# A hybrid GLA and RWKV-7 layer on one core: two small products in fp32 with four column groups, and a new set of precedences

## The chip, the cores and the metric

The kernel runs on one core of a Trainium2 chip. The metric is device time in microseconds (us) of one execution; less is better. The engines carry the profile's names: PE (TensorE: PE the matmuls, PEld the weight loads), DVE (VectorE), ACT (ScalarE), POOL (GpSimd) and SP (SyncE, which only issues DMAs here). SBUF is the on-chip memory of 128 partitions; PSUM holds matmul results, in eight banks of 128 partitions by 512 fp32 numbers.

A *product* below is one matmul instruction: a stationary block of up to 128x128 is loaded, and up to 512 moving columns stream past it. *f32r* is the kernel's fast reading of fp32 numbers, which keeps fewer bits. Where full precision is wanted, the kernel splits a number into a high part and a rest (hi + lo), both f32r, and adds up the products of the parts. An unsplit *fp32* product appears in the trace as two matmul records.

## What is computed

One layer over a prompt of 1024 tokens and eight sample tokens (one new token each for eight sequences), 1024 features. The part of the reference that the change touches:

```python
p = jnp.einsum('btd,dn->btn', x, w_in)
p_gla, p_rwkv, p_gate = _split(p, (GLA_COLS, RWKV_COLS, GATE_COLS))
q, k, v, g_a, a_lr = _split(p_gla, GLA_SPLITS)            # a_lr: 16 columns
log_a = jax.nn.log_sigmoid((jnp.einsum('btr,rk->btk', a_lr, gla_alpha_w2) + gla_alpha_b)
                           .astype(jnp.float32)) / GLA_TAU
...
m = (jax.nn.sigmoid(gate_a) * jnp.einsum('btc,cd->btd', o_gla, w_up_gla)
     + jax.nn.sigmoid(gate_b) * jnp.einsum('btc,cd->btd', o_rwkv, w_up_rwkv))
out = jnp.einsum('btd,de->bte', m, w_out)
y_out = _layernorm(DEEPNORM_ALPHA * x + out, ln_g, ln_b, LN_EPS)
```

`a_lr` is the low-rank factor of GLA's decay: 16 columns of `w_in` applied to x. `out` is the last product, over all prompt and sample tokens. Everything else (the chunked GLA, the RWKV-7 recurrence, gates, norms, states) is there too, and the change leaves it as it is.

## The kernel before

The tokens go through in two passes (`PASS`): pass 0 has 512 prompt tokens and the eight sample tokens, in tiles of 256 and 264 columns; pass 1 has the other 512 in one tile. x lies transposed, as eight blocks (k = 0 to 7) of 128 features by the pass's tokens, each split into `xh` and `xl`. A projection block is 128 output columns: for each tile, 8 blocks k times three f32r products (hi·xh, hi·xl, lo·xh), summed in one PSUM bank. Its weights come through `wraw`, are split by ACT (hi) and DVE or POOL (lo) into `wpart`, and in pass 0 are also written to DRAM, from where pass 1 reads them split.

Behind the projections run the heads and pairs: four GLA heads and eight RWKV pairs in each pass, with many small fp32 matmuls, then two up-projections, a merge and the product with `w_out`. PSUM's banks are named `proj` (2), `big` (5) and `pch` (1). SBUF scratch is mostly the 40 buffers called `row`.

The program is written by a scheduler of its own, `Order`. Each piece of work is a generator (a stream) that yields instructions; `run` keeps an estimated time for each engine and takes the instruction whose estimated start, less a precedence for its kind (`PRIO`, and for PE `FOR_PE`, with the weights `STAND`, `SCARCE`, `PER_ROW`, `URGENT`), is the earliest. `AGE`, `BIAS` and `ASIDE` are further weights in that choice, and `price` gives each instruction an estimated cost. What comes out is one fixed order of instructions for each engine; on the chip the engines wait for each other by semaphores. All instructions are issued by one helper, so most rows of the profile bear the line L227; the tiles' names tell them apart.

Two parts matter here:

- `low_rank` makes `a_lr`. Its weight `wa` (1024x16) is loaded into a `row`, zeroes are written over the final tile, and DVE makes the two parts: of each 128x16 block the stationary has 66 columns, of which 0 to 15 are the high part and 32 to 47 the rest. Each tile takes 16 products, 8 blocks times xh and xl, of 66 columns; ACT or DVE copies rows 0 to 15 of the bank, DVE adds rows 32 to 47, and the sum is split again into `alr` for the heads. It starts when all eight blocks of x are split.
- `out_sample` multiplies the sample rows with `w_out`. ACT gathers xh and xl of the last columns into a 96-column stationary block for each k, and 2 x 16 products of 512 columns run against the two parts of `w_out` (`self.wo`), which `load_out` has split for the prompt's rows. `out_part` adds two strips of the bank, rows 32 to 63 and 64 to 95, to the residual and does the layer norm. In `out` it stands behind the first of four row groups of pass 0; a row group (128 tokens) is 48 products of 512 columns.

A raw block of x is freed as soon as both its parts are made (`low` in `load_x`).

Of the kernel before, what the change touches and what calls it, by code (L numbers as in the profile page):

```python
# [66 lines left out]
RANKW, RANKM = 48, 66  # L67
# [10 lines left out]
AGE = 1.045  # L78
# [3 lines left out]
BIAS = 0.193  # L82
ASIDE = 8.388

PRIO = {"evacuate": 0.39, "pair": 0.3, "turn": 0.5, "chain": 0.42, "norm": 0.1, "x": 0.61, "lora": 0.42, "rank":
        1.25, "head": 0.27, "gate": -0.38, "w": 0.3, "out": 0.04, "state": -0.13, "block": -0.38}
FOR_PE = {"pair": 1.0, "turn": 1.84, "chain": 0.8, "norm": 0.39, "lora": 0.29, "rank": 1.85, "head": 0.89, "gate":
        1.0, "state": 2.11, "out": 0.05}
STAND, SCARCE, PER_ROW = 0.034, 0.249, 0.148

URGENT = 1.707
# [61 lines left out]
def price(eng, name, out, args, ins):  # L153
# [3 lines left out]
    if eng == "P":  # L157
        m = args[0].free_size()
        rows, cols = tiles(name, args)
        if name == "transpose":  # L160
            return 0.1095
        if args[0].dtype == F32R:
            return max(m / 1200, 0.0045 + n / 2256) if rows == cols == P else (m + n) / 1200
        if rows == cols == P:
            return 2 * max(m, n) / 1200 + 0.009
        return 0.1365 if cols == P else (0.0625 if cols == 64 else 0.142 if n > P else 0.088) if rows == P else 0.0625 if rows == cols == 64 else 0.5
# [264 lines left out]
class Kern(Order):  # L431
# [71 lines left out]
    def setup(self):  # L503
# [51 lines left out]
        self.wa = cp.tile([P, NK * RANKW + RANKM - RANKW], F32R, name="wa")  # L555
# [31 lines left out]
    def load_constants(self):  # L587
        a, V, E = self.a, self.V, self.E
        row, wa = yield from self.rows(2)
        wa = wa[:, :NK * 16]  # L590
        yield from self.load("pv", self.S.dma_start(self.pv, a["pv"]))
        yield from self.load("wa", self.S.dma_start(wa, a["wa"]))
# [5 lines left out]
        yield V.tensor_copy(self.wa, row[:, :NK * RANKW + RANKM - RANKW])  # L598
        hi, lo = (self.wa[:, :NK * RANKW].rearrange("p (k c) -> p k c", c=RANKW)[:, :, o:o + 16] for o in (0, 32))
        wa3 = wa.rearrange("p (k c) -> p k c", c=16)  # L600
        yield V.tensor_copy(hi, wa3)
        yield V.tensor_sub(lo, wa3, hi.bitcast(F32))
        self.free(wa)
        self.has.add("wa")
# [21 lines left out]
    def load_x(self, src, i, wait=None, low_rank=False):  # L626
# [5 lines left out]
        self.xq.append(xs)  # L632
        if low_rank:
            self.spawn(self.low_rank(self.ctx[i], xs), "rank")
# [8 lines left out]
        def low():  # L643
            for k in range(NK):
                yield lambda: len(his) > k
                lo = yield from self.get(f"xl{k}")
                yield self.E.tensor_sub(lo[:, :n], raws[k], his[k].bitcast(F32))
                self.free(raws[k])
                xs.append((his[k], lo[:, :n]))
        self.spawn(high(), "x")  # L650
# [149 lines left out]
    def low_rank(self, c, xs):  # L800

        yield lambda: len(xs) == NK and "wa" in self.has
        x_ = yield from self.row(c.n)
        for t0, n in c.tiles:
            q = yield from self.bank("big", [P, n])
            for k in range(NK):
                for v in range(2):
                    yield self.P.matmul(q[:RANKM], self.wa[:, RANKW * k:RANKW * k + RANKM], xs[k][v][:, t0:t0 + n],
                                        start=(k == v == 0), stop=(k == NK - 1 and v == 1))
            x = x_[0:16, t0:t0 + n]  # L810
            yield self.C.copy(x, q[0:16])
            yield self.V.tensor_add(x, x, q[32:48])
# [769 lines left out]
    def load_out(self):  # L1582
# [9 lines left out]
        for k in range(NK):  # L1592
# [21 lines left out]
            self.wo.append([[y.bitcast(F32R) for y in x] for x in parts])  # L1614

    def out(self, c, xs):


        rows = [(n * P, c.i * HT + n * P) for n in range(HT // P)]
        for t0, x0 in rows:  # L1620
            if t0 == P and c.ns:
                yield from self.out_sample(xs)
            fin = t0 == rows[-1][0]
            z, st, done = yield from self.residual(x0, P)
# [26 lines left out]
    def out_sample(self, xs):  # L1651

        W, M = 32, 96
        z, st, done = yield from self.residual(T - W, W)
        xs_ = yield from self.rows(2, NK // 2 * M)
        x3 = [x.bitcast(F32R).rearrange("p (k m) -> p k m", m=M) for x in xs_]
        for k in range(NK):
            yield lambda: len(xs) > k
            y = x3[k // 4][:, k % 4]
            yield self.C.copy(y[:, 0:64], xs[k][0][:, HT + NS - 64:])  # L1660
            yield self.C.copy(y[:, 64:M], xs[k][1][:, HT + NS - W:])
        for j in range(2):
            ps = yield from self.get_of("proj", "big")
            for k in range(NK):
# [4 lines left out]
            if j:  # L1669
                self.free(*xs_)  # L1670
            self.spawn(self.out_part(j, 2, z, j, slice(0, 512), [ps[32:64], ps[64:96]], st, TP, [ps], done), "evacuate")
# [108 lines left out]
    def run_all(self):  # L1780
# [5 lines left out]
        self.plan, self.xq, self.ws, self.wo, self.gts, self.l2s = [], [], [], [], [], []  # L1786
# [71 lines left out]
```

## Time and profile before

| | |
|---|---|
| median of 3 runs | 1460.86 us (1459.19 to 1461.2) |
| span of the profiled execution | 1457.3 us |
| total of the profiled execution | not listed; the median less the span is 3.6 us |
| DMA | 319.14 MB, mean 219 GB/s |
| DVE's costliest group | 191.1 us, 369 adds and products of rows |
| ACT's table loads | 54 in 69.3 us |

The profile gives for each engine the share of the span in which it is busy, and the span in 40 slices with the share in tenths. For a group or a piece of the timeline a row has the start in us and the duration, the engine, the source line, what is written and read (`big<-xh,wa` is a matmul into a `big` bank from `xh` and `wa`), the stationary's size (128*66), the moving operand's size, and the number of merged instructions (x2). In brackets stands how long the engine sat idle before it and what ended that. Matmuls are pipelined: a record's duration reaches into the next one's, so the cost of a stream of matmuls is read from start to start. A row of the windows view has the stretch, its length, then each engine's busy time with its count, the granted PE clock, DMA's share and GB/s.

### The profile page before, as it was taken

How to read it: one execution, taken by the hardware profiler on the slowest of the kernel's cores; microseconds unless marked ns; L12 is line 12 of the kernel's file. 1: busy time of each engine (PE TensorE's matmuls, PEld its weight loads, DVE VectorE, ACT ScalarE, POOL GpSimd, SP SyncE). 2: the span in 40 equal slices, each digit the busy share in tenths (PEclk: the TensorE clock that was granted, in tenths of full speed). 3: DMA queues.
4: the chain of work that ended last, by engine and by line, in shares of the span. 5: the costliest groups of instructions: out<-in, count | busy, mean ns of one | idle time of the engine just before them, and what ended most of it. 6: DMA issues, size and time to landing. Idle time of an engine off the chain costs nothing.

```text
span 1457.3 us, 30477 instructions
## 1 busy us (share of the span) xinstructions
PE 1443.5 (99%) x10768; PEld 1280.5 (88%) x10768; DVE 1058.8 (73%) x2208; ACT 828.9 (57%) x2114; POOL 362.6 (25%) x1111
## 2 busy tenths in 40 slices
PE   9999999999999999999999999999999999999997
PEld 8999999999999998878888888888788898898786
DVE  6687487958895889577747895787669856665665
ACT  5656667766776677455555565464557646643210
POOL 1060506050604160406051405411332330000000
PEclk9999999999999999999999999999999999999999
DMA  8786887678767885675466455746575768798432
GB/s 308 262 289 201 287 275 269 202 245 297 253 209 241 277 307 191 190 210 186 137 205 208 152 173 175 229 138 207 185 230 156 226 206 249 250 311 287 135 119 84
DMA packets 211315, 319.14 MB, mean 219 GB/s; under 512 B 91699, under 2 KB 107196, under 8 KB 211164
## 3 DMA queue, kind: packets, MB, share of 16 engines
q1 hardware_dynamic: 211164, 317.20, 67.6%
q8 instruction: 86, 1.41, 0.4%
q14 instruction: 65, 0.53, 0.1%
HBM read 197.45 MB, written 118.61 MB: 217 GB/s over the span
## 4 chain that ended last, share of the span: by engine, by line
PE 92%; DVE 3%; DMA 3%; ACT 1%; issue 1%; SPq 1%; DVEq 0%; ACTq 0%
PE proj L227 59%; PE big L227 27%; PE pch L227 6%; DVE row L227 1%; SPq L227 1%; DVE xl L227 0%; DMA wraw<-w_in 0%; DMA wide<-LD 0%; DVE wpart L227 0%; DMA row<-xT 0%; DMA wraw<-w_up_gla 0%; DMA row<-o_gla 0%; DMA wide<-Sp 0%; DVE XT L227 0%; DMA w<-wpart 0%
## 5 line engine op out<-in xcount | busy, mean ns | idle before, releaser
L227 PE MATMUL proj<-xh,wpart 128*128 128x264 f32 (+2 forms) x3696 | 901.3, 328 | 0.0
L227 PEld LDWEIGHTS proj<-xh,wpart 128*128 128x128 f32 x3696 | 614.2, 188 | 49.0 <-issue 6.5
L227 PE MATMUL proj<-xl,wpart 128*128 128x264 f32 (+2 forms) x1848 | 603.8, 327 | 0.0
L227 PEld LDWEIGHTS proj<-xl,wpart 128*128 128x128 f32 x1848 | 348.1, 188 | 23.6 <-issue 1.4
L227 POOL TENSOR_TENSOR Xt<-X,wide 128x60 f32<-128x60 f32 (+24 forms) x496 | 170.9, 344 | 676.5 <-DMA wide<-LD 281.4
L227 DVE TENSOR_TENSOR row<-row 128x256 f32<-128x256 f32 (+10 forms) x369 | 191.1, 530 | 14.6 <-ACT row L227 8.0
L227 DVE TENSOR_TENSOR wpart<-wraw,wpart 128x512 fp32r<-128x512 f32 x210 | 146.1, 698 | 74.4 <-ACT wpart L227 71.2
L227 ACT CAST wpart<-wraw 128x512 fp32r<-128x512 f32 x210 | 130.0, 621 | 100.1 <-PE proj L227 57.6
L227 POOL TENSOR_TENSOR X<-X,Xt 128x60 f32<-128x60 f32 (+24 forms) x496 | 170.3, 343 | 38.7
L227 ACT ACTIVATE row<-row 128x520 f32<-128x520 f32 (+4 forms) x229 | 137.7, 612 | 13.3 <-DMA row<-sg 5.6
L227 PE MATMUL big<-xh,wpart 128*128 128x256 f32 (+2 forms) x576 | 133.0, 320 | 0.2 <-DVE wpart L227 0.2
L227 PEld LDWEIGHTS big<-xh,wpart 128*128 128x128 f32 x576 | 95.3, 188 | 7.4 <-DVE wpart L227 0.4
L227 DVE TENSOR_TENSOR wide<-pch,gg 64x65 f32<-64x65 f32 x224 | 49.8, 222 | 65.1 <-PE pch L227 62.9
L227 ACT COPY row<-big 128x128 f32<-128x128 f32 (+6 forms) x152 | 49.7, 356 | 81.1 <-PE big L227 77.0
L227 PE MATMUL big<-xl,wpart 128*128 128x256 f32 (+2 forms) x288 | 92.2, 320 | 0.8 <-DVE xl L227 0.8
L227 DVE SCALAR_TENSOR_TENSOR row<-proj,pv,row 128x255 f32<-128x255 f32 (+1 forms) x95 | 54.6, 575 | 48.2 <-ACT tail L227 36.4
L227 ACT COPY rh<-pch 128x130 f32<-128x130 f32 x121 | 32.5, 268 | 98.8 <-PE pch L227 98.0
L227 ACT COPY wide<-pch 64x65 f32<-64x65 f32 x241 | 50.1, 208 | 50.4 <-PE pch L227 47.4
L227 ACT ACTIVATE row<-proj,omu 128x256 f32<-128x256 f32 (+1 forms) x95 | 52.2, 549 | 33.5 <-PE proj L227 32.5
L409 ACT ACT_TABLE_LOAD x54 | 69.3, 1283 | 0.9
L227 PE MATMUL big<-row 128*64 128x64 f32 (+4 forms) x648 | 65.0, 272 | 0.2 <-DVE gg L227 0.2
L227 PEld LDWEIGHTS big<-xl,wpart 128*128 128x128 f32 x288 | 54.2, 188 | 5.3 <-DVE xl L227 1.8
(234 smaller groups left out, 2069.6 us busy)
## 6 DMA issues: line engine op xcount, KB each, us to landing
w<-wpart SPq DMA_DIRECT2D x146, 512.0 KB, 4.3
wpart<-w SPq DMA_DIRECT2D x146, 512.0 KB, 3.8
wraw<-w_in SPq DMA_DIRECT2D x146, 256.0 KB, 4.2
wide<-LD SPq DMA_DIRECT2D x64, 128.0 KB, 3.8
wraw<-w_up_gla SPq DMA_DIRECT2D x32, 256.0 KB, 3.7
wraw<-w_up_rwkv SPq DMA_DIRECT2D x32, 256.0 KB, 3.7
sg<-row SPq DMA_DIRECT2D x16, 260.0 KB, 3.2
row<-sg SPq DMA_DIRECT2D x16, 260.0 KB, 4.3
```

Of the source, the lines that this page charges most:

```text
L227: ways.append((eng, lambda call=call: call(out, *args, **kw), price(eng, name, out, args, ins)))
L409: self.nc.scalar.preload_act_table_set(self.table)
```

## The change

Four things change.

`low_rank` works on unsplit fp32: `wa` is loaded straight into its tile, with 16 columns a block, and the moving operand is the raw block of x. Block k goes to column group k mod 4, that is to rows 0, 32, 64 or 96 of the bank, so four products stand in four groups of 32 columns of the array, and a second four adds to them. The four strips are then summed, by one copy and three adds. Pass 0 issues both tiles in one piece, once all eight raw blocks are there, into two `proj` banks; pass 1 issues two pieces of four blocks, into a `big` bank that it takes at its start. A raw block of x is freed only when low rank has used it.

```diff
-        self.wa = cp.tile([P, NK * RANKW + RANKM - RANKW], F32R, name="wa")
+        self.wa = cp.tile([P, NK * RANK], F32, name="wa")
...
-        yield V.tensor_copy(self.wa, row[:, :NK * RANKW + RANKM - RANKW])
...
-        yield V.tensor_copy(hi, wa3)
-        yield V.tensor_sub(lo, wa3, hi.bitcast(F32))
...
-    def low_rank(self, c, xs):
-
-        yield lambda: len(xs) == NK and "wa" in self.has
+    def low_rank(self, c, raws, ranked):
+
         x_ = yield from self.row(c.n)
-        for t0, n in c.tiles:
-            q = yield from self.bank("big", [P, n])
-            for k in range(NK):
-                for v in range(2):
-                    yield self.P.matmul(q[:RANKM], self.wa[:, RANKW * k:RANKW * k + RANKM], xs[k][v][:, t0:t0 + n],
-                                        start=(k == v == 0), stop=(k == NK - 1 and v == 1))
-            x = x_[0:16, t0:t0 + n]
-            yield self.C.copy(x, q[0:16])
-            yield self.V.tensor_add(x, x, q[32:48])
+        step = NK if c.i == 0 else 4
+        qs = []
+        for _, n in c.tiles:
+            qs.append((yield from self.bank("big" if c.i else "proj", [P, n])))
+        for k0 in range(0, NK, step):
+            yield lambda: len(raws) >= k0 + step and "wa" in self.has
+            yield together([self.P.matmul(q[g:g + RANK], self.wa[:, RANK * k:RANK * k + RANK], raws[k][:, t0:t0 + n],
+                                          start=(k < 4), stop=(k >= NK - 4), skip_group_check=True)
+                            for q, (t0, n) in zip(qs, c.tiles) for k in range(k0, k0 + step) for g in [k % 4 * 32]])
+            ranked[k0:k0 + step] = [True] * step
+        for q, (t0, n) in zip(qs, c.tiles):
+            x = x_[0:RANK, t0:t0 + n]
+            yield self.C.copy(x, q[0:RANK])
+            for g in range(32, P, 32):
+                yield self.V.tensor_add(x, x, q[g:g + RANK])
             self.free(q)
```

The sample rows do the same: `sample_rows` adds xh and xl of 32 columns back to fp32, the eight blocks are stationary in four groups, and `w_out` is loaded a second time, raw, in two halves of eight `row` buffers (`self.wr`). The sample rows now stand behind two row groups of pass 0 in place of one.

```diff
+        for j in range(2):
+            raws = yield from self.rows(NK, 512)
+            for k in range(NK):
+                yield self.S.dma_start(raws[k], self.a["w_out"][k * P:(k + 1) * P, 512 * j:512 * j + 512])
+            self.wr.append(raws)
...
-            if t0 == P and c.ns:
-                yield from self.out_sample(xs)
...
+            if t0 == 2 * P and c.ns:
+                yield from self.out_sample(ys)
...
-            for k in range(NK):
-                yield lambda: len(self.wo) > k
-                for v in range(2):
-                    yield self.P.matmul(ps[:M], x3[k // 4][:, k % 4], self.wo[k][v][j], start=(k == v == 0),
-                                        stop=(k == NK - 1 and v == 1))
...
+            qs = [ps[g:g + W] for g in range(0, P, W)]
+            yield together([self.P.matmul(qs[k % 4], ys[1][:, k], raws[k], start=(k < 4), stop=(k >= 4), skip_group_check=True)
+                            for k in range(NK)])
```

`price` gets a cost for the new form, and the precedences and weights get new values, two of them here:

```diff
-AGE = 1.045
+AGE = 1.137
...
-URGENT = 1.707
+URGENT = 1.514
```

So the order of all engines is laid out anew, and it differs at nearly every place behind the first 50 rows of PE. The following rows are of PE, at the three places of low rank and the sample rows (a row: line, operation, written and read tiles, size of the result; the number in `xh_239` counts tiles).

PE at the start, before the change: the first two projection blocks go through x block by block, and low rank's 66-column products stand behind eight of the twelve products of block 4 (six are left out here).

```order
L227 MATMUL big<-xh_237,wpart 128x264
L227 MATMUL big<-xh_252,wpart 128x256
L227 MATMUL big<-xl_264,wpart 128x256
...
L227 MATMUL big<-xh_200,wa 66x256
L227 MATMUL big<-xl_205,wa 66x256
```

PE at the same place in the change:

```order
L229 MATMUL big<-xl_255,wpart 128x264
L229 MATMUL big<-xh_239,wpart 128x264
L229 MATMUL proj<-row,wa 16x256 x8
L229 MATMUL proj<-row,wa 16x264 x8
L229 MATMUL big<-xh_254,wpart 128x256
```

Low rank moved ahead of block 4 (`xh_252` before, `xh_254` now), and its two tiles stand together.

PE at the turn from pass 0 to pass 1, before the change: low rank stands among the projections of pass 1, 16 products in one piece, of which the first three and the row behind the last are shown.

```order
L227 MATMUL proj<-xh_9051,wpart 128x512
L227 MATMUL big<-xh_8997,wa 66x512
L227 MATMUL big<-xl_8999,wa 66x512
L227 MATMUL big<-xh_9005,wa 66x512
...
L227 MATMUL big<-part,headsr 128x512 x2
```

The change, at the first and at the second half, 167 rows apart:

```order
L229 MATMUL big<-row 64x64 x12
L229 MATMUL big<-row,wa 16x512 x4
L229 MATMUL big<-part,headsr 128x512 x2
...
L229 MATMUL proj<-xh_9026,wpart 128x512
L229 MATMUL big<-row,wa 16x512 x4
L229 MATMUL proj<-xh_9042,wpart 128x512
```

The first half moved into the last projection block of pass 0 (tiles of 256 and 264 columns), the second among the first of pass 1.

PE at the sample rows, before the change (`gg`, `wide`, `row`, `part`, `lw` and `wpart` are the places of `w_out`'s parts):

```order
L227 MATMUL big<-wpart,xl_18363 128x512
L227 MATMUL proj<-gg,row 96x512 x4
L227 MATMUL proj<-wide,row 96x512 x4
L227 MATMUL proj<-row 96x512 x4
L227 MATMUL proj<-part,row 96x512
L227 MATMUL proj<-lw,row 96x512
L227 MATMUL proj<-wpart,row 96x512 x2
```

And in the change, where they come one row group later:

```order
L229 MATMUL proj<-wpart,xh_18323 128x512 x2
L229 MATMUL proj<-wpart,xl_18336 128x512
L229 MATMUL big<-row 32x512 x16
L229 MATMUL proj<-gg,xh_18249 128x512 x2
L229 MATMUL proj<-gg,xl_18251 128x512
```

The 32 products of 96 columns became 16 of 32 columns, in one row of the order. On SP, 16 loads of `w_out` stand behind the loads of the first four blocks of x for pass 1's output, 13 of them ahead of the residual's rows for the second row group and three behind.

More of the change, by code (lines that the diff above doesn't have):

```diff
@@ L66 @@
 IDLE = 3
[L67 removed]
+RANK = 16
 SPARE_ROWS = 11
@@ L76 @@
 TABLE = 1.28
-AGE = 1.045
+AGE = 1.137
 SPARE = 0.411
 LANDED = 0.648
[L82 to L89, printed above, removed]
-URGENT = 1.707
+BIAS = 0.197
+ASIDE = 6.466
+PRIO = {"evacuate": 0.333, "pair": 0.3, "turn": 0.5, "chain": 0.42, "norm": 0.1, "x": 0.642, "lora": 0.42,
+        "rank": 1.201, "head": 0.27, "gate": -0.38, "w": 0.3, "out": -0.09, "state": 0.199, "block": 0.227}
+FOR_PE = {"pair": 1.0, "turn": 1.562, "chain": 0.8, "norm": 0.591, "lora": 0.821, "rank": 2.048,
+          "head": 0.89, "gate": 1.0, "state": 2.877, "out": 0.355}
+STAND, SCARCE, PER_ROW = 0.034, 0.109, 0.06
+URGENT = 1.514
 SIGMOID, EXP = "sigmoid_and_others", "natural_log_exp_and_others"
@@ L165, in price @@
             return 2 * max(m, n) / 1200 + 0.009
+        if cols == 32 and n > 2 * P:
+            return 0.017 + n / 2326
         return 0.1365 if cols == P else (0.0625 if cols == 64 else 0.142 if n > P else 0.088) if rows == P else 0.0625 if rows == cols == 64 else 0.5
@@ L588, in load_constants @@
         a, V, E = self.a, self.V, self.E
-        row, wa = yield from self.rows(2)
-        wa = wa[:, :NK * 16]
+        row = yield from self.row()
         yield from self.load("pv", self.S.dma_start(self.pv, a["pv"]))
-        yield from self.load("wa", self.S.dma_start(wa, a["wa"]))
+        yield from self.load("wa", self.S.dma_start(self.wa, a["wa"]))
+        self.has.add("wa")
         yield V.memset(row, 1.0)
@@ L632, in load_x @@
         self.xq.append(xs)
+        ranked = [not low_rank] * NK
         if low_rank:
-            self.spawn(self.low_rank(self.ctx[i], xs), "rank")
+            self.spawn(self.low_rank(self.ctx[i], raws, ranked), "rank")
         def high():
@@ L647, in low, with done @@
                 yield self.E.tensor_sub(lo[:, :n], raws[k], his[k].bitcast(F32))
-                self.free(raws[k])
                 xs.append((his[k], lo[:, :n]))
+                if low_rank:
+                    self.spawn(done(k), "x")
+                else:
+                    self.free(raws[k])
+        def done(k):
+            yield lambda: ranked[k]
+            self.free(raws[k])
         self.spawn(high(), "x")
```

36 lines of the change are left out of this document (19 added, 17 removed).

## The prediction

> **What bounds the kernel now.** I read the page's table of busy shares first, then its row of granted clock, then PE's waits, then PE's timeline at the places that the change touches.
>
> ```profile
> span 1457.3 us, 30477 instructions
> PE 1443.5 (99%) x10768; PEld 1280.5 (88%) x10768; DVE 1058.8 (73%) x2208; ACT 828.9 (57%) x2114; POOL 362.6 (25%) x1111
> PEclk9999999999999999999999999999999999999999
> PE 92%; DVE 3%; DMA 3%; ACT 1%; issue 1%; SPq 1%; DVEq 0%; ACTq 0%
> ```
>
> PE is busy for 1443.5 of 1457.3 us, at full clock in every slice, and the chain that ended last is 92% PE. The next engine, DVE, has a quarter of the span to spare. So time on PE is time of the kernel, and work taken off DVE, ACT or SP is worth something only where PE waits for it. Those waits, all of them over the whole span:
>
> ```profile
> PE big L227 <- DVE wa L227: 1.4, 1, 1.4
> PE pch L532 <- DVE warm L529: 1.1, 1, 1.1
> PE big L227 <- DVE gg L227: 0.9, 3, 0.3
> PE big L227 <- DVE xl L227: 0.8, 3, 0.4
> PE big L227 <- DVE S L227: 0.8, 2, 0.4
> PE big L227 <- DMA wraw<-w_up_gla: 0.4, 1, 0.4
> PE pch L227 <- DMA wide<-Sp: 0.4, 1, 0.4
> PE big L227 <- DVE row L227: 0.2, 1, 0.2
> PE big L227 <- DVE wpart L227: 0.2, 1, 0.2
> ```
>
> They sum to 6.2 us (columns: us in total, times, longest). The largest is a wait for `wa`, the weight whose split the change removes. The table tells a second thing: a new order has about 4.6 us to win at most, and everything it makes PE wait is lost.
>
> **What is removed.** The low-rank factor's three tiles and the sample rows, each by its first matmul and by the next one of other work:
>
> ```profile
> 14.02 0.28 PE L227 MATMUL big<-xl,wpart 128*128 128x256 f32 x1
> 15.71 0.33 PE L227 MATMUL big<-xh,wa 128*66 128x256 f32 x1 [1.41 <-DVE wa L227]
> 17.63 0.40 PE L227 MATMUL big<-xh,wpart 128*128 128x256 f32 x2
> 18.84 0.31 PE L227 MATMUL big<-xh,wa 128*66 128x264 f32 x1 [0.21 <-DVE row L227]
> 20.80 0.28 PE L227 MATMUL big<-xh,wpart 128*128 128x264 f32 x1
> 575.23 0.39 PE L227 MATMUL big<-xh,wa 128*66 128x512 f32 x1
> 578.91 0.63 PE L227 MATMUL big<-part,headsr 128*128 128x512 f32 x2
> 1364.35 1.08 PE L227 MATMUL proj<-gg,row 128*96 128x512 f32 x4
> 1371.77 0.63 PE L227 MATMUL big<-gg,xh 128*128 128x512 f32 x2
> ```
>
> The durations in these rows overlap, since a matmul starts before the one ahead has drained, so I count from start to start: 1.92 + 1.96 us for pass 0 (16 products each), 3.68 for pass 1 (16), 7.42 for the sample rows (32). Together **14.98 us** for 80 products.
>
> **What is added.** 16 + 8 + 16 fp32 products of a 128x16 or 128x32 stationary block, four of them side by side in four column groups. The trace has one such form already, the sample part of a GLA head:
>
> ```profile
> 167.64 0.28 PE L227 MATMUL proj<-xl,wpart 128*128 128x256 f32 x1
> 167.85 0.64 PE L227 MATMUL big<-row 128*32 128x256 f32 x8
> 168.42 0.49 PE L227 MATMUL pch<-wide 128*128 128x130 f32 x2
> 324.24 0.39 PE L227 MATMUL proj<-xh,wpart 128*128 128x256 f32 x1
> 324.47 0.28 PE L227 MATMUL proj<-xl,wpart 128*128 128x256 f32 x1
> 324.59 0.40 PE L227 MATMUL proj<-xh,wpart 128*128 128x256 f32 x2
> 135.78 0.59 PE L227 MATMUL big<-row 128*128 128x256 f32 x2
> 136.22 0.39 PE L227 MATMUL pch<-wide,gg 128*128 128x130 f32 x2
> ```
>
> Eight records are four products: an fp32 product has two. All eight take 0.57 us from the first start to the next work (167.85 to 168.42). One full-width fp32 product of 256 columns, in the last two rows, takes 0.44 us for its two records. So four products in four groups cost hardly more than one alone: they do run beside each other, where one after another the 40 new ones would take 24 x 0.88 + 16 x 0.45 = 28.3 us. A burst of four at 256 columns lies between 0.44 us (streaming alone) and 0.57 us (drained each time). I take 0.48, nearer the lower end, because part of the 0.13 us between them is the way out of the mode, which a row of bursts pays once. At 264 columns that is 0.49. At 512 columns it is 2 x 0.44 = 0.88 plus the 0.04, so 0.92, an estimate, for which the trace has no row; its upper end, with a drain each time, is 0.88 + 0.13 = 1.01.
>
> - Pass 0: two bursts per tile, 2 x 0.48 + 2 x 0.49 = 1.94 us (1.76 to 2.28).
> - Pass 1: two bursts, 1.84 us. Sample rows: four bursts, 3.68 us. (Together 5.28 to 6.06.)
>
> That is 7.46 us. Each visit to this mode costs something at its edges: in, 167.64 to 167.85 is 0.21 where the next f32r matmul of 256 columns comes after 0.12 (324.47 to 324.59), so 0.09; out, 0.57 - 0.48 = 0.09; and the first f32r product behind it takes 0.23 (324.24 to 324.47), 0.11 more. That is 0.29 us a visit. By the order shown with the change there are four (pass 0 in one, pass 1 in two, the sample rows in one): 1.16 us. Added in all: **8.6 us** (7.0 to 9.5). Net on PE: 14.98 - 8.6 = **6.4 us less** (5.5 to 8.0).
>
> At this place the Trainium skill speaks against the change. "TensorE: Matmul & The Clock Gate", section "Measured speedup vs the span model", gives 3.07 times for four packed tiles and 2.38 for three, short of the full factor. By it the 28.3 us would become 9.2 and not 7.46, an estimate, and the net 4.6. The trace's burst gives 4 x 0.44 / 0.57 = 3.1 when it stands alone, so it agrees for one burst with its way out; no run here shows several in a row.
>
> **The wait at the start.** The wait of 1.41 us is for the split of `wa` into two parts on DVE. The change loads `wa` as it is, and PE needs only its landing:
>
> ```profile
> 8.27 0.33 SPq L227 DMA_DIRECT2D row<-wa  x1
> row<-xT SPq DMA_DIRECT2D x8, 260.0 KB, 5.0
> 11.10 2.01 ACT L227 CAST xh<-row 128x520 fp32r<-128x520 f32 x3
> 14.23 0.62 DVE L227 CAST wa<-row 128x402 fp32r<-128x402 f32 x2
> 14.77 0.68 DVE L227 TENSOR_TENSOR wpart<-wraw,wpart 128x512 fp32r<-128x512 f32 x1
> ```
>
> `wa` is issued at 8.27 us behind the last row of xT; such a row lands 5.0 us after its issue, so `wa` by some 13.3, an estimate, and the cast at 14.23, which needs it, waits for nothing. The last raw rows of x are read by ACT from 11.10 on, so they have landed before 13.1. In the new order the low-rank products stand eight products earlier, ahead of block 4 of x, at about 13.2 us (14.02 less seven products of 0.12). Both inputs are there or nearly so by then, and the wait goes; if `wa` landed as late as its cast, some 1 us of it would stay. What is late next is the fourth weight part, which DVE makes at 14.77 to 15.45 today; in the new order DVE comes to it sooner, having no `wa` to split, and PE first needs it six products behind low rank, at 13.2 + 2.2 + 0.7 = 16.1. The second wait of 0.21 (for the first tile's DVE copy, which held the bank) goes too, since both tiles now have a bank at once. **1.6 us** (0.6 to 1.9).
>
> **What I cost at nothing.** Three adds instead of one per tile on DVE, eight small adds and four more partial sums for the sample rows, 16 fewer ACT copies and six fewer table loads: DVE and ACT are waited for only in the list above. The sample rows' sums come with two more rows of output ahead of the end; such a row is 48 products at 7.42 / 32 = 0.23 us, so 11 us of PE:
>
> ```profile
> 1312.00:1348.00 36.00, 36.00 (x157) 29.16 (x156) 20.20 (x33) 13.38 (x22) 0.00 (x0) 1.00 0.87 288
> 1449.49 0.28 PE L227 MATMUL big<-wpart,xl 128*128 128x256 f32 x1
> ```
>
> The 16 further loads of w_out are 4.2 MB. They are issued behind the first four rows of the second half's x, some 4 us into the first row of output, and take 14.6 us at the 288 GB/s of the busy stretch above; two rows of output, 22 us, cover that, and some 4 us are left. Without that cover PE would wait for what is missing. The last matmul starts at 1449.49 and the span ends 7.8 us later; that tail is the same code.
>
> The new order: counted over both programs, PE changes between kinds of matmul (width of block or fp32 against f32r) 1136 times before and 1139 after, eight of these being the four new visits. So apart from them it changes five times fewer, at some 0.1 us each: 0.5 us, which I leave in the range. The waits may move either way; I take 0, within 2 us down and 4 up.
>
> **Sum.** 1457.3 - 6.4 - 1.6 = 1449.3 us of span. The profiled execution's own total isn't listed, so I take the median less the span, 1460.86 - 1457.3 = 3.6 us, as what lies around it: **1452.8 us**, 0.55% less.
>
> **Rivals.**
> 1. *The gain at the start is given back.* The first 36 us move data at 0.87 of DMA's share:
>
> ```profile
> 24.75 0.28 PE L227 MATMUL proj<-xh,wpart 128*128 128x256 f32 x1
> 0.00:36.40 36.40, 33.21 (x256) 32.44 (x257) 24.51 (x61) 20.83 (x45) 4.22 (x15) 1.00 0.87 308
> ```
>
> Pass 0's gain is 1.6 + 3.88 - 1.94 - 0.29 = 3.25 us, so the third block starts at 21.5 us and not at 24.75. If weights come no faster than they do now, PE then waits for the next part and all of that goes, which leaves 4.8, or 1456.1 us. For it: the share. Against it: PE waited for `wpart` only 0.2 us.
> 2. *Every burst drains*, as the traced ones do with their way out: 2.28 + 6.06 + 1.16 = 9.5 us, a net of 5.5, 1453.8 us. For it: no row shows two bursts in a row. Against it: nothing in a second burst changes the mode. The page's factor named above is this case; by it alone the time would be 1454.7.
> 3. *The new order waits more than the old*, by 5 to 8 us spread over the passes: 1458 to 1461, no change. For it: PE's order differs throughout, and the old one waits little. Against it: with 1443.5 us busy there has nearly always been a projection to run.
> 4. *Slower: a bank held at the turn of the passes.* In pass 1 low rank takes its `big` bank before x is there and keeps it between its halves, 167 rows of PE's order, at 1457.3 / 7668 = 0.19 us a row some 32 us. A pair's front takes four of the five `big` banks at once, so while one is held, fronts, heads and transposes take turns. If projections run out meanwhile (their x changes over at just that place), PE idles. At a third of those 32 us the kernel loses 10.7 and ends at 1463.5; it decides from 8.0 us of new idle on. For it: the place. Against it: no wait of PE in the whole list but those at the start is over 0.4 us.
> 5. *The groups don't overlap at 512 columns*, and the change doesn't do what it says: 1457.3 + 28.3 + 1.2 - 15.0 - 1.6 + 3.6 = 1473.8. The break-even lies at an overlap of 28.3 / 15.4 = 1.8. Against it: 0.57 us for four.
>
> **Chances.** Forecast with its own spread (1449 to 1455): 0.56. Rival 1: 0.10. Rival 2: 0.14. Rival 3: 0.11. Rival 4: 0.05. Rival 5: 0.02. A new order that is better by over 4 us: 0.02. A measurement of this kernel tells apart about 0.2%, 2.9 us, so under 1457.9 counts as faster: 0.56 + 0.10 + 0.14 + 0.02 and the lower part of rival 3, 0.84 in all; same 0.11; slower 0.05. The range takes in rivals 1 and 2, and below, the cheapest bursts, the five changes fewer and some waits: 1448.5 to 1457.5.
>
> **What would show it.** In the profile of the change: no wait for `wa`, and the third block's first product near 21.5 us; bursts of eight records in 0.9 us at 512 columns, the sixteen sample products in 3.7 to 4.1 us where 7.42 stood; PE's waits in sum under 6 us; the last matmul near 1441. I am wrong if the bursts take over 1.1 us, if PE's waits grow by several us at the turn of the passes (rival 4), or if PE waits for `row<-w_out` ahead of the sample rows.

## The result, and the profile after

| | before | change |
|---|---|---|
| median | 1460.03 us (4 runs, 1459.09 to 1461.2) | 1450.12 us (4 runs, 1449.43 to 1451.64) |
| profiled execution, total / span | not listed / 1457.3 us | 1450.79 / 1448.9 us |
| change over before | | **0.9934** (95%: 0.992 to 0.9948) |

The change is faster by 0.66%, which is 9.6 us of 1460 (7.6 to 11.7 by the interval). Around the span of the change lie 1.9 us, and 1.7 to 2.2 in the profiled executions of all runs below. So the profiled execution of before, whose total isn't listed, took about 1459.2 us, by this estimate the shortest of its first three runs (1459.19).

The first parts of the change's page:

```profile
span 1448.9 us, 30483 instructions
PE 1434.9 (99%) x10768; PEld 1268.1 (88%) x10768; DVE 1067.0 (74%) x2237; ACT 816.2 (56%) x2078; POOL 365.9 (25%) x1111
PEclk9999999999999999999999999999999999999999
```

PE still sets the time. Its busy time fell by 8.6 us and the span by 8.4; what it idles stayed at 14 us. PE's waits in the change (columns as before):

```profile
PE big L229 <- DVE S L229: 2.2, 5, 0.6
PE pch L534 <- DVE warm L531: 1.1, 1, 1.1
PE pch L229 <- DVE wide L229: 0.6, 2, 0.3
PE pch L229 <- POOL wide L229: 0.5, 1, 0.5
PE big L229 <- DMA row<-OS: 0.5, 1, 0.5
PE big L229 <- DVE xl L229: 0.4, 1, 0.4
PE big L229 <- DVE gg L229: 0.3, 1, 0.3
PE big L229 <- DVE wpart L229: 0.2, 1, 0.2
PE proj L229 <- DVE xl L229: 0.2, 1, 0.2
```

The wait for `wa` is gone, and the sum is 6.0 us where it was 6.2. Other small waits have come in its place. The new products on PE's timeline, with the row behind each, the first product of the third block, and the last matmul:

```profile
13.23 0.28 PE L229 MATMUL big<-xh,wpart 128*128 128x264 f32 x1
13.44 1.95 PE L229 MATMUL proj<-row,wa 128*16 128x256 f32 x32
15.31 0.38 PE L229 MATMUL big<-xh,wpart 128*128 128x256 f32 x1
15.54 0.28 PE L229 MATMUL big<-xl,wpart 128*128 128x256 f32 x1
21.18 0.28 PE L229 MATMUL proj<-xh,wpart 128*128 128x256 f32 x1
545.03 1.05 PE L229 MATMUL big<-row,wa 128*16 128x512 f32 x8
546.01 0.73 PE L229 MATMUL big<-part,headsr 128*128 128x512 f32 x2
570.68 1.85 PE L229 MATMUL big<-row,wa 128*16 128x512 f32 x8
572.46 0.50 PE L229 MATMUL proj<-xh,wpart 128*128 128x512 f32 x1
1370.70 3.64 PE L229 MATMUL big<-row 128*32 128x512 f32 x32
1374.27 0.73 PE L229 MATMUL proj<-gg,xh 128*128 128x512 f32 x2
1441.07 0.28 PE L229 MATMUL big<-wpart,xl 128*128 128x256 f32 x1
```

From start to start, pass 0's two tiles (32 records, 16 products) take 1.87 us, pass 1's two pieces 0.98 and 1.78, the sample rows 3.57. That is 8.20 us where 14.98 stood. The lead over before grows at the three places of the change: the third block starts at 21.18 us in place of 24.75, 3.6 us earlier; the first product with `w_out` at 1348.37 in place of 1353.24, 4.9 us earlier, with pass 1's low rank in between; and the last matmul, behind the sample rows, 8.4 us earlier.

One of these is twice as long as its twin: the second piece of pass 1, 1.78 us against 0.98. The weight loads of that place say why:

```profile
570.68 0.12 PEld L229 LDWEIGHTS big<-row,wa 128*16 128x16 f32 x6 [0.37 <-issue]
571.49 0.11 PEld L229 LDWEIGHTS big<-row,wa 128*16 128x16 f32 x2 [0.69 <-DMA row<-xT]
```

Six loads, three of the four products, go at once. The last product's waits 0.69 us for its raw block of x. Idle time in PE's own row doesn't show it, since the other three groups were still streaming. The late block belongs to this one execution, and not to the change. lowrank_only, a run below with the same order up to the sample rows, has the second piece and the row behind it here:

```profile
569.93 1.05 PE L229 MATMUL big<-row,wa 128*16 128x512 f32 x8
570.91 0.51 PE L229 MATMUL proj<-xh,wpart 128*128 128x512 f32 x1
```

That is 0.98 us, as for the first piece, and old_rest, old_pe, old_prio and state_only have 0.98 as well. Only old_prec shows the wait again (0.67 us).

### The profile page after: what moved, and what is told of

The parts are those of the page before. It is cut to its first block, busy times and chain, and to the rows that moved or that the text cites. A ratio compares the mean times of both kernels' runs of the same rounds, so it can differ in the third digit from the quotient of the medians.

```text
span 1448.9 us, 30483 instructions
## 1 busy us (share of the span) xinstructions
PE 1434.9 (99%) x10768; PEld 1268.1 (88%) x10768; DVE 1067.0 (74%) x2237; ACT 816.2 (56%) x2078; POOL 365.9 (25%) x1111
## 3 DMA queue, kind: packets, MB, share of 16 engines
q8 instruction: 86, 1.41, 0.4%
## 5 line engine op out<-in xcount | busy, mean ns | idle before, releaser
L229 PE MATMUL proj<-xh,wpart 128*128 128x512 f32 (+2 forms) x3696 | 900.0, 327 | 0.0
L229 PE MATMUL proj<-xl,wpart 128*128 128x512 f32 (+2 forms) x1848 | 604.9, 327 | 0.2 <-DVE xl L229 0.2
L229 DVE TENSOR_TENSOR row<-row 128x256 f32<-128x256 f32 (+9 forms) x369 | 190.4, 528 | 16.6 <-ACT row L229 9.5
L229 POOL TENSOR_TENSOR X<-X,Xt 128x60 f32<-128x60 f32 (+24 forms) x496 | 174.4, 352 | 38.6
L229 ACT ACTIVATE row<-row 128x520 f32<-128x520 f32 (+3 forms) x229 | 138.4, 611 | 10.9 <-DMA row<-sg 4.5
L229 PE MATMUL big<-row 128*64 128x64 f32 (+5 forms) x680 | 68.3, 287 | 0.3 <-DVE gg L229 0.3
```

The costliest lines, as they stand in the source:

```text
L229: ways.append((eng, lambda call=call: call(out, *args, **kw), price(eng, name, out, args, ins)))
```

## Experiments

All are the change or the kernel before with one edit. Ratios are over the kernel before, run in the same job.

| run | what differs | median, us | ratio (95%) |
|---|---|---|---|
| lowrank_only | the change, sample rows as before | 1452.84 | 0.9958 (0.9944 to 0.9971) |
| old_prec | the change, all precedences and weights as before | 1469.49 | 1.0072 (1.006 to 1.0085) |
| new_prec | before, precedences and weights of the change | 1506.95 | 1.0326 (1.0312 to 1.034) |
| sample_only | new_prec and the change's sample rows | 1500.85 | 1.0284 (1.027 to 1.0298) |
| one_piece | the change, pass 1's low rank in one piece | 1454.92 | 0.9978 (0.997 to 0.9987) |
| same_neighbours | one_piece, other order inside the pieces | 1453.91 | 0.9971 (0.9961 to 0.998) |
| one_group | the change, all new products in one column group | 1505.26 | one run |
| late_rank | before, low rank behind the first blocks | 1509.53 | one run, before 1460.38 |
| old_pe | the change, PE's own precedences as before | 1452.05 | 0.9947 (0.9932 to 0.9962) |
| old_prio | the change, `PRIO` as before | 1470.9 | 1.0079 (1.0062 to 1.0096) |
| old_rest | the change, `AGE`, `BIAS`, `ASIDE`, `URGENT` as before | 1449.66 | 0.9932 (0.9917 to 0.9946) |
| state_only | old_prio with one number of the change's | 1475.28 | 1.0104 (1.0088 to 1.0121) |

### The products, one part at a time

**Low rank alone.** The change with `load_out`, `out` and `out_sample` of before:

```diff
-            if t0 == 2 * P and c.ns:
-                yield from self.out_sample(ys)
+            if t0 == P and c.ns:
+                yield from self.out_sample(xs)
```

> The change with the sample rows as before (96-column f32r products on the split w_out, behind the first row group, no second loading of w_out). Theory W: the change less what the sample rows gained in its trace (7.42 us became 3.8): 1450.1 + 3.6 = 1453.7 us, within 2 us; the first plain product of the third block stays at about 21.2 us. Rival O: as the change, 1450 us.

It ran in 1452.84 us, as theory W said. Its order is that of the change on every engine up to the sample rows and the second loading of `w_out`. By the ratios the sample rows are worth 0.9958 - 0.9934 of 1459 us, 3.5 us, give or take 2.8. The two traces say it more closely: the last product ahead of them starts at 1357.12 us here and at 1359.24 in the change, the last matmul of all at 1442.55 and 1441.07, so from a lead of 2.1 us this run falls 1.5 behind, which is 3.6 us. The prediction's terms give 7.42 - 3.68 - 0.29 = 3.45. The other 6.1 us (4.2 to 8.2) are low rank, its wait, and the new order; the prediction's terms give 7.56 - 1.94 - 1.84 - 0.87 + 1.6 = 4.5, inside that interval. Where the other 1.6 us come from isn't shown.

**The sample rows alone, under the new numbers.** Before, with the change's sample rows, precedences and price:

> The kernel before with the sample rows of the change and the new precedences; low rank stays split, with 66 columns. Theory W: 1460.0 - 3.6 = 1456.4 us, within 2 us; the third block still starts at 24 to 25 us and the wait for wa is still there (1.4 us) unless the new order happens to place it later. Rival O: 1450 to 1453 us.

It is 41 us slower than before, but so is its base, new_prec (below). Theory W's 1456.4 us and Rival O's 1450 to 1453 both fail. Against that base it gains 0.0042 of 1459, 6.1 us (give or take 2.9), with its 16 products in 3.57 us, as in the change. Its order differs from its base, so what lies beyond 3.5 us can't be put down to the products. The timeline keeps the wait for the split weight, as it should:

```profile
16.14 0.34 PE L229 MATMUL big<-xh,wa 128*66 128x256 f32 x1 [1.68 <-DVE wa L229]
```

**All in one column group.** The change with every new product in rows 0 to 15, or 0 to 31, of its bank; the sums over strips fall away:

```diff
-                                          start=(k < 4), stop=(k >= NK - 4), skip_group_check=True)
-                            for q, (t0, n) in zip(qs, c.tiles) for k in range(k0, k0 + step) for g in [k % 4 * 32]])
+                                          start=(k == 0), stop=(k == NK - 1), skip_group_check=True)
+                            for q, (t0, n) in zip(qs, c.tiles) for k in range(k0, k0 + step) for g in [0]])
```

> The change with all products of low rank and the sample rows in one column group (the strips' adds fall away, since there is one strip). If the overlap of four groups is what makes the fp32 form cheap: eight products of 256 columns take 3.5 us and eight of 264 3.6 us in pass 0 (1.87 us for both tiles in the change), pass 1's two pieces 3.5 us each (0.98 and 1.78), the sample rows 14.1 us (3.57). Rival (a product of 16 or 32 columns is cheap by itself): less than half of these. The order behind the start differs from the change, so the whole time isn't compared; with the order kept it would be 20 us more.

Timeline of PE at the first visit, and the groups of the other two (busy time behind the bar):

```profile
13.45 7.19 PE L229 MATMUL proj<-row,wa 128*16 128x256 f32 x32
20.57 0.39 PE L229 MATMUL big<-xh,wpart 128*128 128x256 f32 x1
```

```profile
L229 PE MATMUL big<-row 128*32 128x512 f32 x32 | 13.9, 593 | 0.0
L229 PE MATMUL big<-row,wa 128*16 128x512 f32 x16 | 7.2, 593 | 0.0
```

The same 16 products take 7.12 us in one group and 1.87 in four, and the sample rows 13.9 and 3.57: the four groups work **3.8 to 3.9 times** as fast. Rival 5 falls, and so does the run's own rival, that such narrow products are cheap by themselves. The whole time is not the price of these products: they cost some 20 us more, the time rose by 55, and the order is another one.

**One piece in pass 1, and the order inside a piece.** In both runs one number changes when pass 1's low rank may start, `step = NK`. The second run also lets two products of the same group follow each other, here in low rank and in the same way in the sample rows:

```diff
-for k in range(k0, k0 + step) for g in [k % 4 * 32]])
+for k in [k0, k0 + 4, k0 + 1, k0 + 5, k0 + 2, k0 + 6, k0 + 3, k0 + 7] for g in [k % 4 * 32]])
```

> The change with pass 1's low rank in one piece of eight blocks in place of two of four. Theory R (in the change the second half waits 0.7 us for its last raw block of x, which comes just before it): the eight products of pass 1 take 1.8 us in one visit, against 0.98 + 1.78 us in two, if the planner places them behind the last block's landing; the time falls by about 1.2 us, if the order elsewhere waits no more than in the change: 1448 to 1451 us. Rival: a piece that has to have all eight blocks comes late and holds the raw rows and the bank longer, so projections or pairs wait: 1452 us or more, with new waits of PE between 545 and 600 us.

> As the run in one piece, but inside each piece the products are issued as blocks 0, 4, 1, 5, 2, 6, 3, 7, so that two neighbours always go to the same column group; results, data and the order around them stay the same. Theory G (groups overlap only where the neighbours in issue order go to different groups): of four products only two run together, so pass 0 takes 3.5 us in place of 1.9, pass 1 3.5 in place of 1.8 and the sample rows 7.0 in place of 3.6: about 6.8 us more than the run in one piece. Rival Q (each group has a queue of its own, so the order inside a piece doesn't matter): 1.9, 1.8 and 3.6 us as they were, and the time of the run in one piece within 1 us.

Timeline of one_piece at the turn of the passes:

```profile
570.32 0.50 PE L229 MATMUL big<-part,headsr 128*128 128x512 f32 x1 [0.34 <-ACT part L229]
571.96 0.50 PE L229 MATMUL big<-part,headsr 128*128 128x512 f32 x1 [1.14 <-DVE part L229]
573.88 1.91 PE L229 MATMUL big<-row,wa 128*16 128x512 f32 x16
```

and of same_neighbours:

```profile
573.82 1.93 PE L229 MATMUL big<-row,wa 128*16 128x512 f32 x16
```

In one piece the eight products take 1.84 us (to 575.72), exactly the prediction's term for both halves. With lowrank_only's 0.98 this shows that the 1.78 of the change's second half was its late block of x and nothing in the array. Yet the kernel got slower, 0.9978 against 0.9934, some 6.4 us (give or take 2.4): theory R falls and the rival's time holds. At this place 1.5 us of new waits show; the order behind it is another, and the rest was not followed up. The neighbours make next to no difference, with every engine's order of work otherwise the same: from start to start 1.88 and 1.90 us in pass 0, 1.84 and 1.86 here, 3.57 and 3.61 for the sample rows. Rival Q is right and theory G wrong. A second product of one group, issued next to the first, doesn't hold up the products of the other groups behind it: the first four still start together, within 0.04 us of each other (0.02 in one_piece).

**The wait for `wa`, taken away alone.** Before, with pass 0's low rank held until the first two blocks are issued:

```diff
-        yield lambda: len(xs) == NK and "wa" in self.has
+        yield lambda: len(xs) == NK and "wa" in self.has and (c.i or self.begun)
```

> The kernel before, with low rank of pass 0 held back until the first two projection blocks are issued; products and weights as before. Theory W (the wait for the split of wa was PE time of its own, 1.6 us, and the shorter products gave the other 2.0 of the 3.6 us by which the third block starts earlier in the change): PE waits for nothing at 14 to 16 us and its first two blocks end 1.6 + 3.9 = 5.5 us earlier than in the kernel before, so that low rank starts at about 19.3 us; low rank itself takes 3.9 us as before, wherever it stands. Rival (something else, such as the fourth weight part, holds PE at that place as well): the blocks end later than 20.5 us, with a new wait in the place of the old one.

PE's timeline at that place, and the third block's first product:

```profile
15.60 0.50 PE L227 MATMUL big<-xh,wpart 128*128 128x256 f32 x2 [1.04 <-DVE wpart L227]
20.52 0.28 PE L227 MATMUL proj<-xh,wpart 128*128 128x256 f32 x1
```

and DVE's:

```profile
14.32 0.62 DVE L227 CAST wa<-row 128x402 fp32r<-128x402 f32 x2
14.86 0.68 DVE L227 TENSOR_TENSOR wpart<-wraw,wpart 128x512 fp32r<-128x512 f32 x1
```

The rival is right: 1.04 of the 1.41 us came back under another name. DVE makes the fourth weight part behind the cast of `wa`, and PE, no longer held by low rank, came to it earlier and ran into that. So moving the product is not enough. (The whole run took 49 us more than before, with another order and new waits behind the start, so only the start is compared.) In the change DVE makes that part here:

```profile
14.45 0.68 DVE L229 TENSOR_TENSOR wpart<-wraw,wpart 128x512 fp32r<-128x512 f32 x1
```

PE comes to it six products behind low rank, at about 16.1 us, a whole us after it is made. Even at late_rank's time, 15.54, it would have been there. So the change meets neither wait, for two reasons: low rank reads `wa` as it was loaded, and low rank's own 1.87 us stand ahead of the products that need the fourth part.

### The numbers that set the order

**Old numbers on the new products, and new numbers on the old ones.**

```diff
-AGE = 1.137
+AGE = 1.045
...
-STAND, SCARCE, PER_ROW = 0.034, 0.109, 0.06
+STAND, SCARCE, PER_ROW = 0.034, 0.249, 0.148
...
-URGENT = 1.514
+URGENT = 1.707
```

> The change with the old precedences and weights. Theory W (the gain is matmul work taken off PE, some 5.9 us, and the wait of 1.6 us for the split of wa; the order gives nothing that lasts): 1449 to 1454 us, the low-rank and sample stretches as short as in the change (1.9 us in pass 0, 3.6 us for the sample rows), and no wait for wa. Rival O (the new precedences make the gain): 1457 to 1461 us.

> The kernel before with the new precedences and weights, its products as they were. Theory W: 1457 to 1463 us, no faster than the kernel before by more than its waits allow (4.6 us at the very most). Rival O: 1450 to 1454 us.

In both runs both theories fell. With the old numbers the change is **slower than before**, though its products are as short as in the change (low rank 1.95, 2.9 in pass 1; sample rows 1.9 + 1.9). The old kernel with the new numbers loses 48 us. The largest wait of PE in each, first old_prec, then new_prec:

```profile
PE pch L229 <- DVE row L229: 4.6, 1, 4.6
```

```profile
PE proj L227 <- ACT xh L227: 13.8, 3, 11.5
```

So the 0 us that the new order costs in the change holds for this program with these numbers. It isn't a property of the numbers, nor of the products. Since the order follows from both, no run here has the new products in the old order.

**Which numbers?** Three parts of the table, each put back alone:

> The change with the old values of PE's own precedences alone (FOR_PE, STAND, SCARCE, PER_ROW). The change with all old values took 19 us more than the change, most of it where the last pairs' chains ran at the end of pass 1 with too little other matmul work left. Theory P (PE's precedences decide how much projection work is kept for that end): 1460 to 1470 us, again with waits of pch at 1150 to 1220 us. Theory T (any one set of old values lays out another order, and each costs something): 1452 to 1460 us, and the same of the other two sets.

> The change with the old values of PRIO alone (the precedences on DVE, ACT, POOL and SP). Theory P: 1449 to 1454 us, no new waits at the end of pass 1. Theory T: 1452 to 1460 us.

> The change with the old AGE, BIAS, ASIDE and URGENT alone. Theory P: 1449 to 1454 us. Theory T: 1452 to 1460 us.

Theory P falls: PE's own precedences and weights are worth 2 us (0.9947 against 0.9934, intervals overlapping) in place of 10 or more, and `PRIO` alone brings back a loss as large as that of old_prec, though its largest hole is another one. Theory T falls too: its 1452 to 1460 us fit old_pe alone, since the four plain numbers are worth nothing and `PRIO` 21 us. In old_prio the largest hole of PE is here (timeline, then windows: stretch, length, PE busy, granted clock, DMA share, GB/s):

```profile
1270.20 0.58 PE L229 MATMUL proj<-xh,wpart 128*128 128x256 f32 x1 [6.60 <-ACT xh L229]
```

```profile
1200.00:1300.00 100.00, 90.62 (x575) 0.93 0.72 233
...
1272.00:1276.00 4.00, 3.08 (x12) 0.50 1.04 376
```

Of these 100 us PE is idle for 9.4 in old_prio; in the change the same stretch is busy throughout.

The product behind the hole belongs to the second up-projection, over the RWKV outputs `o_rwkv`, and its x comes late. Why, the transfers of `OS` tell: the sample tokens' RWKV result, which must be stored and read again before `o_rwkv` is complete. First old_prio (first and last start stand behind the durations):

```profile
L229 SPq DMA_DIRECT2D row<-OS x8: 280/294/323, 1251.1 to 1255.3; - x8
L229 SPq DMA_DIRECT2D row<-o_rwkv x16: 319/426/1703, 1266.4 to 1321.9; - x16
```

then the change:

```profile
L229 SPq DMA_DIRECT2D row<-OS x8: 263/294/329, 980.5 to 984.1; - x8
L229 SPq DMA_DIRECT2D row<-o_rwkv x16: 428/432/1273, 1227.4 to 1302.0; - x16
```

In the change the sample result is there 240 us ahead; in old_prio it comes at 1251 us, and the reads of `o_rwkv` start 39 us later. The stream that makes it has the precedence `state`, -0.13 before and 0.199 in the change. So the last run puts that number alone into old_prio:

```diff
-"state": -0.13, "block": -0.38}
+"state": 0.199, "block": -0.38}
```

> The old precedences (PRIO) of the kernel before, run with the change's products, with one of them, "state", put back to the change's 0.199 from -0.13; the other five stay old. Theory S: that one number carries the loss of old_prio (1470.9 us), because it sets when the sample row of the recurrent state is updated: in the trace of old_prio its result is stored at 1247.7 us and the blocks that read it come after 1251.1, while the change stores at 973.9 and reads from 980.5. By S the time is 1449 to 1455 us, the store comes before 1100 us, and the 9.6 us that TensorE loses near 1260 to 1280 in old_prio are gone. Rival M: the loss is in the mixture of the six, or in another of them ("out", "x", "evacuate", "block", "rank"): the store moves forward all the same, since "state" sets it, and the time stays at 1464 to 1472 us. Between 1455 and 1464: both.

Transfers of state_only:

```profile
L229 SPq DMA_DIRECT2D row<-OS x8: 286/293/318, 987.5 to 992.6; - x8
L229 SPq DMA_DIRECT2D row<-o_rwkv x16: 320/430/1404, 1231.1 to 1320.6; - x16
L229 SPq DMA_DIRECT2D o_rwkv<-row x17: 320/369/1921, 204.2 to 1309.3; - x17
```

and its timeline at its two largest holes behind 1300 us:

```profile
1317.82 0.51 PE L229 MATMUL big<-xh,wpart 128*128 128x512 f32 x1 [3.03 <-ACT xh L229]
1376.99 0.79 PE L229 MATMUL big<-wpart,xh 128*128 128x512 f32 x1 [4.88 <-ACT wpart L229]
```

Rival M is right about the cause, though at 1475.28 us the time lies above its range. `state` does set when the sample result comes (987.5 us, as in the change), and the reads start at 1231 again. But the time is no better: PE idles at other places. The recurrence of the last pairs now ends late, the last `o_rwkv` block is stored at 1309.3 us (the change: 1268.7), and PE waits for x in the same up-projection, 48 us further on. At 1377 us a part of `w_out` is late: ACT, which makes it, sat idle 5.5 us for the transfer `row<-w_out`. So the time hangs on several seams of the order at once. Theory S named a real cause of one hole and took it for the cause of the loss. Which of the other five numbers of `PRIO` holds back the recurrence and the load was not tried.

## Why the prediction was right, step by step

The forecast was 1452.8 us, in a range of 1448.5 to 1457.5; it came out at 1450.12.

- **Removed products**, 14.98 us: all gone. lowrank_only bears out the sample rows' share, 3.6 us net by the traces against 3.45.
- **Added products**, 7.46 us: 8.20. Pass 0 took 1.87 (predicted 1.94), the first piece of pass 1 0.98 (0.92), the sample rows 3.57 (3.68). The one term that is off is the second piece of pass 1: 0.92 predicted, 1.78 measured. The prediction took both pieces as bursts whose inputs are there. The weight loads show a late raw block in this execution; with the block there, lowrank_only has 0.98 at the same place and one_piece 1.84 for all eight. By the letter of the prediction's own sign of being wrong, bursts over 1.1 us, this piece counts against it; but it waited, and its groups overlapped.
- **Edges**, 1.16 us for four visits: what lies outside the stretches above (the way in, as 13.23 to 13.44 less 0.12; the first f32r product behind, as 15.31 to 15.54 less 0.12) comes to some 0.2 us at three visits and 0.1 at 545 us, where other fp32 work stands ahead, 0.7 in all; the way out lies inside them. Added is thus 8.9 us, against 8.6.
- **Rival 2 and the factor of the Trainium skill.** Had each burst drained, the sample rows had taken four times 1.01, 4.04 us; they took 3.57. One after another the 40 products were estimated at 28.3 us and measured in one_group at 7.12 + 7.2 + 13.9 = 28.2. The Trainium skill's factor in "TensorE: Matmul & The Clock Gate", section "Measured speedup vs the span model", 3.07 for four tiles (there row tiles), is too low for such a row of bursts: 3.8 to 3.9 here, and the measurement decides.
- **The wait at the start**, 1.6 us: gone, and the third block came at 21.18 us (predicted 21.5). The fourth weight part came sooner, as said (14.45 in place of 14.77), but that wasn't needed: by the prediction's own 16.1 us PE comes to it late enough either way, and late_rank shows what happens where low rank doesn't stand ahead of it. Rival 1 fell: the weights kept pace, and of the 3.57 us of this place nothing was lost later (4.9 us at the first product with `w_out`).
- **The order**, 0 us: PE's waits 6.0 us against 6.2, none at the turn of the passes from 540 to 580 us and 0.5 just behind (rivals 3 and 4). The value was right, but nothing in the prediction derives it: that this order costs nothing was luck as far as its working goes. The other tunings of the same products cost 0 to 25 us in the runs above, far beyond the bound of 4 us, and the argument against rival 3, that there has nearly always been a projection to run, doesn't hold for them.
- **The sum.** In span 1449.3 was predicted, 1448.9 measured; 14.98 - 8.9 + 1.6 = 7.7 us are accounted for of the 8.4 that it fell, and 0.7 are not. (Two profiled runs with the same order, the change's and lowrank_only's, differ by 2.1 us ahead of the sample rows, 0.8 of them by the late block, so a match this close is in part luck too.) What made the predicted total 2.7 us too high is mainly the last step, **the 3.6 us around the span**: they were the median of three runs less the span of another, shorter execution. Only 1.9 us lie around a span, which is 1.7 of the 2.7; 0.4 are the span, and 0.7 the median of the change, which lies below its profiled execution.
- **The chances.** Rival 5's 0.02 was counted under "same", though its 1473.8 us would be slower: 0.09 and 0.07 would have been right in place of 0.11 and 0.05.

## What to carry to other kernels

Where PE was 99% busy, here, start-to-start intervals of the nearest rows priced a swap of products to within a microsecond; check for each new piece that its last input is there, since a wait of one column group can hide from PE's idle time. Before removing a wait, look at what PE comes to next: late_rank only traded it for another, and the change met neither, since its low rank needs no split and still stands ahead of the next part that is made late. A tuned table of numbers belongs to the program that it was tuned with: price a change with the order that it will run in, and don't expect one number to carry the effect of the table.

## What the runs showed of the hardware

- Four column groups run beside each other even where two products of one group stand next to each other in the order: eight products of 512 columns take 1.84 us with the groups in turn and 1.86 in pairs, against 7.2 us for the same eight in one group. So a product that must wait for its group doesn't hold up those of other groups behind it. (That three groups went ahead while the fourth waited 0.69 us in the change's second piece doesn't show this, since the fourth was the last in the order.)
- Idle time of PE costs more than itself. After 6.6 us of it in old_prio the granted clock was 0.50 for some 12 us (1268 to 1280), and products of 256 columns had records of 0.58 us in place of 0.28. Over the whole run PE idled 9.6 us more than in the change (1468.2 - 1444.6 against 1448.9 - 1434.9 us), and was busy 9.7 us longer with the same number of matmuls. Some 6 of these 9.7 us are the clock, an estimate from the 12.4 us of busy PE that stood at 0.50 (9.0 here, 3.4 from 1154 to 1157 us); the rest isn't explained. The Trainium skill, "TensorE: Matmul & The Clock Gate", section "What's actually happening", has the clock fall to half after an idle window of about 3.4 us. The runs agree in part: the change, whose longest wait is 1.1 us, keeps full speed in every slice, and behind the waits of 4.6 us (old_prec) and 6.6 us it was at 0.50. But it also fell where PE never sat idle that long: to 0.50 behind waits of 2.06 and 3.03 us in state_only, and in old_prec behind three waits of 0.35 us in a row, with PE busy for 0.60 to 0.65 of each us from 1149 to 1152. Two stretches of 1 us there, from that part and from what followed:

```profile
1150.00:1151.00 1.00, 0.61 (x3) 1.00 1.03 197
...
1153.00:1154.00 1.00, 1.00 (x6) 0.50 0.94 299
```

So it isn't enough to look for one long wait: here some 3 us in which PE was busy for 60% were followed by 3.4 us at half clock (1152.3 to 1155.7).
